# Convolution taps on TensorE, rotation tables from angles, and three projections as plain fp32 products

## The chip, the cores and the metric

The kernel runs on one core of one Trainium2 chip. Times are device microseconds (us) of that core, from the profiler or from timed runs; lower is better. The engines named here: PE is TensorE (matrix products; PEld is its weight loading, which overlaps), DVE is VectorE, ACT is ScalarE, POOL is GpSimd, and SP is SyncE, which issues nearly all transfers. TensorE runs at one of two clock levels, 1.2 and 2.4 GHz; the profile gives the granted clock of each stretch as a share of the higher one.

## The reference, cut to what matters

Two transformer blocks run one after the other on 256 tokens of 1024 features, in fp32.

```python
# block 1, first mixer
h = rmsnorm(x, norm_mix_g)
q, k, v, f, u_ssm, g_attn, g_ssm = split(h @ w_in)      # 512, 512, 512, 8, 512, 1024, 1024
q, k = rmsnorm(q per head), rmsnorm(k per head)
y_attn = forgetting_attention(q, k, v, f)                # 8 heads of 64
y_ssm  = s5(u_ssm, A, log_dt, B, C, D, w_glu)            # x_t = exp(A dt) x_{t-1} + Bbar u_t; y = Re(C x) + D u
x = x + (sigmoid(g_attn) * (y_attn @ w_proj_attn) + sigmoid(g_ssm) * (y_ssm @ w_proj_ssm)) @ w_out
x = x + moe(rmsnorm(x))                                  # 32 experts, top 2
# block 2, layer 0
u = x @ conv_w_in                                        # 768 values, 768 gates, 256 memory queries
h = a * sigmoid(gate)                                    # 768 channels
h = causal depthwise convolution of h, 31 taps per channel, + dw_b
y = concat(silu(layer_norm(h)), memory_attention(q_mem)) @ w_o[0]
x = layer_norm(alpha * x + y); x = layer_norm(alpha * x + moe(x))
# block 2, layer 1: the same with a blockwise causal attention in place of the convolution
```

## The kernel before, in words

The stages follow each other: first mixer (0 to about 265 us), experts of block 1, convolution layer (about 539 to 690 us), its experts, attention layer, its experts. A tile framework orders the instructions of each engine when the kernel is compiled: in program order where nothing waits, and otherwise by what its own cost model takes to be ready. `issue_after` adds an order that it has to keep.

**Weights.** All weights come as 1 MB slots of a ring, in the order of one plan, loaded by SP in order (`pump`, `take`, `done`): five slots while the first mixer's state space work is live, thirteen after it. A slot is loaded again when `done` has given it back. With `K.borrow = n` the next n slots given back are not loaded again but kept in `K.kept`.

**Split products.** The mixers' projections split each fp32 operand into a high and a low fp32r part and make three fp32r products of it (`mm3`, L165 to L167): high by high, high by low, low by high. `split_half` (L137 to L143) splits half a slot: ACT copies the high part, then DVE (L143) or, for the halves numbered in the set `POOL`, GpSimd (L141) subtracts. `dense(n)` announces 2n halves; three pairs of buffers hold the split halves.

**First mixer (`Mixer1.run`).** The transposed input times the norm gain gives `xg`, which is split into `L`. Then come the projections in the order u (state space input), q, k, v (`in_proj`, four halves each, 16 pairs of k tile and token tile, 48 products of 512 columns each), with the per-head norms of q and k on ACT and DVE and their transposes on PE (L1314). `s5_lanes` works out the powers of the state transition on DVE from dt and A, and is put behind the last split of the q projection. `s5_weights(hf)` (hf 0 or 1, half of the groups) builds the input and output matrices (DVE and POOL) and the table `tab` of cos and sin of n times an angle, n from 0 to 63: it starts from two columns and doubles five times, each time with two complex products on DVE (12 instructions, L991 to L996). Half 0's tables are built ahead of the loop, half 1's in it. The loop (about 94.5 to 212 us) takes steps of the gate projections (split products), of the state space scan and of the attention in the order of a fixed string (`M1_ORDER`). `split_rows` splits a block of gain rows on POOL (L1516 to L1522), ahead of the loop.

**Convolution layer (`conv`).** The projection goes in 14 halves (`col_proj`, L1707 to L1709, 24 products of 256 columns each): values and gates of channel tiles 0 and 1, of 2 and 3, then the memory queries, then tiles 4 and 5. Of the six tiles of 128 channels, `ASG = 'vgmmmv'` gives two to DVE (31 instructions of one tap each, L1803), one to POOL (L1814 to L1823), and three to PE: `stack` builds diagonal weight blocks from the taps, `shift` writes the tile to DRAM and reads it back four times, shifted by one token each, into a kept ring slot (L1840, L1843), and `taps_pe` makes 32 small products (L1850). A memory attention of four heads runs in the same stretch; `CONV_ORDER` fixes the order of steps. Then follow a layer norm over the channels and the output projection (`out_proj`, split products), where the low part of each finished tile is subtracted on POOL (L1966).

Of the kernel before, what the change touches and what calls it, by code (L numbers as in the profile page):

```python
# [21 lines left out]
class Core:  # L22
# [165 lines left out]

    def out_proj(self, L, order, outs):
# [90 lines left out]
POOL = {2, 4, 13, 17, 18, 23, 26, 27, 31, 32, 33, 38, 42, 44, 45, 50, 52, 53, 56, 64, 65, 68, 71, 72, 73, 74, 76, 79, 84, 86, 87, 90, 94, 95, 97, 98}  # L280
# [687 lines left out]
class Mixer1:  # L968
# [29 lines left out]
    def s5_lanes(self):  # L998
# [22 lines left out]
        v.scalar_tensor_tensor(an, n, -P2, an, op0=OP.mult, op1=OP.add)  # L1021
        v.tensor_scalar(an, an, 3.1415925, -3.1415925, op0=OP.min, op1=OP.max)
# [35 lines left out]
        self.bb, self.sn = bb, sn  # L1058
# [13 lines left out]
    def s5_weights(self, hf):  # L1072
# [32 lines left out]
        c, s = self.tab[:, 0], self.tab[:, 1]  # L1105
        v.memset(c[:, :, 0:1], 1.0)
        v.memset(s[:, :, 0:1], 0.0)
        v.tensor_copy(c[:, :, 1:2], self.sn[:, 3, ps, None])
        v.tensor_copy(s[:, :, 1:2], self.sn[:, 2, ps, None])
        n = 2  # L1110
        d1, d2 = t1.rearrange("p a b c -> p (a b c)"), t2.rearrange("p a b c -> p (a b c)")
        ph = sp.tile([128, 2, 8], FT, name="s_ph")
        while n < 64:

            p_ = [z[:, :, n - 1] for z in (c, s)]
            o_ = [z[:, :, 1] for z in (c, s)]
            self.cmul(v, ph[:, 0], ph[:, 1], p_[0], p_[1], o_[0], o_[1], d1[:, :8], d2[:, :8])
            f = [ph[:, i, :, None].to_broadcast([128, 8, n]) for i in range(2)]
            e = [z[:, :8 * n].rearrange("p (a b) -> p a b", a=8) for z in (d1, d2)]
            self.cmul(v, c[:, :, n:2 * n], s[:, :, n:2 * n], c[:, :, :n], s[:, :, :n], f[0], f[1], e[0], e[1])  # L1120
            n *= 2
# [125 lines left out]
    def run(self, close, spare):  # L1247
# [25 lines left out]
        K.dense(16)  # L1273
        o = K.bank2()
        run(K.in_proj(L, o))
# [11 lines left out]
        qn = T("qn", [128, 2, 512], tag="m_u")  # L1287
        hs, hr = T("hs", [128, 2, 8]), T("hr", [128, 2, 8])
# [194 lines left out]
class Block2:  # L1483
# [30 lines left out]
    def split_rows(self):  # L1514
        g, r = self.K.nc.gpsimd, self.rtmp
        g.tensor_copy(self.rows, r)  # L1516
        g.tensor_sub(r, r, self.rows)
        for i in range(1, 3):
            o = slice(32 * i, 32 * i + 32)
            g.tensor_copy(self.rows[o], r[o])  # L1520
        g.tensor_sub(r[o], r[o], self.rows[o])
        g.tensor_copy(self.rows[o], r[o])  # L1522
# [249 lines left out]
    def conv(self, L, mp):  # L1772
# [20 lines left out]
        def taps(c, lo=0, hi=31, o=None, first=True):  # L1793

            o = cT[c] if o is None else o
            for w in range(lo, hi):
                h = hT[:, c, w:w + 256]
                if w == 0:
                    v.tensor_scalar(o, h, dw(c, 0), col(c), op0=OP.mult, op1=OP.add)
                elif w == lo and first:  # L1800
                    v.tensor_scalar(o, h, dw(c, w), None, op0=OP.mult)
                else:
                    v.scalar_tensor_tensor(o, h, dw(c, w), o, op0=OP.mult, op1=OP.add)  # L1803
                if (w - lo) % 4 == 3:
                    yield

        def taps_pool(c, hi):

            o, u = cT[c], B[:, 1]
            for w in range(0, hi, 4):  # L1810
                n = min(4, hi - w)
                h = hT[:, c, w:w + 256]
                h = bass.AP(tensor=h.tensor, offset=h.offset, ap=[list(h.ap[0]), [1, n], [1, 256]])
                g.tensor_tensor(u[:, :n], h, self.dw[:, 31 * c + w:31 * c + w + n, None].to_broadcast([128, n, 256]), op=OP.mult)  # L1814
                if n == 4:
                    g.tensor_tensor(u[:, 0:2], u[:, 0:2], u[:, 2:4], op=OP.add)
                    n = 2
                for j in range(1, n):
                    g.tensor_tensor(u[:, 0], u[:, 0], u[:, j], op=OP.add)
                if w:  # L1820
                    g.tensor_tensor(o, o, u[:, 0], op=OP.add)
                else:
                    g.tensor_scalar(o, u[:, 0], col(c), None, op0=OP.add)  # L1823
                yield
# [37 lines left out]
        def project():  # L1862
            for i in range(4):
# [291 lines left out]
```

## Time and profile before

| what | us |
|---|---|
| median of 3 runs (1815.61 to 1818.11) | 1817.23 |
| the profiled execution, its own time | 1819.84 |
| its span, first to last instruction | 1818.0 |
| PE busy, share of the span | 1636.8 (90%) |
| DVE busy | 711.5 (39%) |
| ACT busy | 439.6 (24%) |
| POOL busy | 227.9 (13%) |
| weights read | 539.23 MB, 297 GB/s over the span |

The shares are averages over stages with different limits: in the expert stages PE is busy nearly throughout, while in the first mixer and in the convolution layer PE, DVE and POOL take turns in waiting for each other. Matmuls overlap in the array, so a busy PE is not a PE at its peak. In the views a releaser is the instruction whose end let a waiting one start.

### The profile page before, as it was taken

Reading aid. Unit: us, or ns where it says so; the run is one execution under the profiler, and the core shown is the slowest. Engines: PE = TensorE matmul, PEld = TensorE weight load, DVE = VectorE, ACT = ScalarE, POOL = GpSimd, SP = SyncE. Lnnn points to the kernel's source line nnn. Section 1 sums busy time; section 2 is a strip of 40 time slices with the busy share of each in tenths; the row PEclk is TensorE's granted clock in tenths of the full one; section 3 lists DMA queues with packets and bytes.
Section 4 is the critical chain, followed back from the end, with each engine's and each line's share of the span. In section 5 each row is a group of like instructions: output and inputs, shape, how many; then the busy total and the mean of one; then the engine's idle time right before and its main releaser. Section 6 shows DMA issues by size and latency. Waiting matters only on the chain. (4 is left out here: it accounts for less than half of the span.)

```text
span 1818.0 us, 28309 instructions
## 1 busy us (share of the span) xinstructions
PE 1636.8 (90%) x11151; PEld 986.3 (54%) x11153; DVE 711.5 (39%) x1688; ACT 439.6 (24%) x859; POOL 227.9 (13%) x151
## 2 busy tenths in 40 slices
PE   6689888999957778999999999699799999999995
PEld 5477667888847554444444443598444444444442
DVE  6988764233337973111111111554611111111113
ACT  4244342222223351111111111355211111111111
POOL 4525110000017420000000000322000000000000
PEclk9799899989979889999999999899899999999998
DMA  7222566989991536998899999734199999879970
GB/s 291 93 92 79 199 257 270 419 350 419 419 372 63 173 116 257 422 421 357 353 421 421 421 421 421 267 121 139 71 387 419 419 419 420 348 280 420 397 296 26
DMA packets 77565, 543.43 MB, mean 299 GB/s; under 512 B 8861, under 2 KB 11037, under 8 KB 12216
## 3 DMA queue, kind: packets, MB, share of 16 engines
q1 hardware_dynamic: 77224, 540.75, 74.3%
q8 instruction: 130, 2.13, 0.5%
q14 instruction: 67, 0.55, 0.1%
q10 hardware_dynamic: 144, 0.00, 0.0%
HBM read 539.23 MB, written 1.49 MB: 297 GB/s over the span
## 5 line engine op out<-in xcount | busy, mean ns | idle before, releaser
L564 PE MATMUL ps<-ring,bA 128*32 128x128 f32 (+1 forms) x3336 | 455.9, 440 | 4.5 <-DMA ring<-in_gu_dram 2.0
L564 PEld LDWEIGHTS ps<-ring,bA 128*32 128x32 f32 (+1 forms) x3336 | 162.0, 124 | 204.0 <-issue 176.3
L615 PE MATMUL ps<-ring,bF 128*64 128x512 f32 (+1 forms) x1248 | 217.1, 523 | 1.1 <-ACT bA L1556 0.6
L635 PE MATMUL d<-w,bB 128*128 128x256 f32 (+1 forms) x1016 | 206.8, 350 | 2.2 <-ACT w L625 2.2
L635 PEld LDWEIGHTS d<-w,bB 128*128 128x128 f32 x1016 | 154.6, 189 | 78.8 <-issue 49.7
L626 DVE SCALAR_TENSOR_TENSOR w<-ps,cs,w 128x512 fp32r<-128x512 f32 (+1 forms) x95 | 62.8, 661 | 286.0 <-ACT w L625 285.9
L615 PEld LDWEIGHTS ps<-ring,bF 128*64 128x64 f32 (+1 forms) x1248 | 74.7, 128 | 125.0 <-issue 108.9
L511 POOL CAST bD<-bC 128x1024 bf16<-128x1024 f32 (+1 forms) x17 | 20.2, 1191 | 931.6 <-PE ps L548 827.0
L599 DVE COPY bF<-ps 128x256 f32<-128x256 f32 x63 | 26.8, 425 | 276.5 <-PE ps L597 276.5
L625 ACT ACTIVATE w<-ps,cs 128x512 fp32r<-128x512 f32 (+1 forms) x95 | 58.4, 615 | 268.2 <-PE ps L615 268.2
L554 ACT ACTIVATE bB<-ps 32x256 fp32r<-32x256 bf16 (+1 forms) x127 | 47.6, 375 | 275.7 <-PE ps L548 260.7
L526 PE MATMUL ps<-bC,L 128*128 128x256 f32 x640 | 95.7, 297 | 11.9 <-PEq L655 7.6
L526 PEld LDWEIGHTS ps<-bC,L 128*128 128x128 f32 x640 | 88.1, 202 | 24.8 <-PEq L655 17.5
L528 ACT ACTIVATE bA<-ps 128x512 f32<-128x512 f32 x80 | 47.8, 597 | 200.5 <-PE ps L526 197.4
L137 ACT ACTIVATE W<-ring 128x1024 fp32r<-128x1024 f32 x66 | 69.4, 1056 | 110.1 <-PE d L167 39.4
L580 DVE SCALAR_TENSOR_TENSOR bE<-bE,ps 128x256 f32<-128x256 f32 (+1 forms) x95 | 33.6, 353 | 147.7 <-ACT bE L579 145.5
L166 PE MATMUL d<-W,L 128*128 128x512 f32 (+1 forms) x176 | 71.4, 406 | 21.7 <-DVE W L143 21.7
L141 POOL TENSOR_TENSOR W<-ring,W 128x1024 fp32r<-128x1024 f32 x27 | 65.9, 2445 | 148.8 <-ACT W L137 113.0
L165 PE MATMUL d<-W,L 128*128 128x512 f32 (+1 forms) x176 | 72.3, 415 | 11.8 <-ACT W L137 11.3
L579 ACT ACTIVATE bE<-ps 128x256 f32<-128x256 f32 (+1 forms) x95 | 31.3, 329 | 192.3 <-PE ps L564 192.3
L564 PE MATMUL ps<-W,bA 128*64 128x512 f32 (+1 forms) x472 | 70.4, 445 | 1.7 <-PEq L655 1.0
L167 PE MATMUL d<-W,L 128*128 128x512 f32 (+1 forms) x176 | 70.5, 402 | 0.0
(519 smaller groups left out, 2338.9 us busy)
## 6 DMA issues: line engine op xcount, KB each, us to landing
ring<-in_gu_dram SPq DMA_DIRECT2D x246, 1024.0 KB, 14.0
ring<-in_dn_dram SPq DMA_DIRECT2D x126, 1024.0 KB, 12.5
W<-in_gu_dram SPq DMA_DIRECT2D x38, 1024.0 KB, 13.7
x<-in_gu_dram SPq DMA_DIRECT2D x20, 1024.0 KB, 12.5
W<-in_dn_dram SPq DMA_DIRECT2D x17, 1024.0 KB, 13.0
ring<-in_w_in_dram SPq DMA_DIRECT2D x16, 1024.0 KB, 5.9
ring<-in_w_moba_dram SPq DMA_DIRECT2D x10, 1024.0 KB, 19.8
x<-in_dn_dram SPq DMA_DIRECT2D x9, 1024.0 KB, 17.0
```

Source lines behind the costliest of these rows:

```text
L137: copy = self.nc.scalar.activation(hi, s, AF.Copy)
L141: self.nc.gpsimd.tensor_sub(lo, s, hi)
L165: mm(out, lh, rh, start=start, stop=False, skip_group_check=True)
L166: mm(out, lh, rl, start=False, stop=False, skip_group_check=True)
L167: mm(out, ll, rh, start=False, stop=stop, skip_group_check=True)
L526: nc.tensor.matmul(p[:, i * n:i * n + n], x[:, t, k0 + i, :], g[t], start=s == 0, stop=s == 3)
L528: nc.scalar.activation(xg[:, k0:k0 + per, :], p[:, :per * n].rearrange("p (k c) -> p k c", k=per), AF.Copy)
L564: self.mm = nc.tensor.matmul(p[C * j:C * j + C, :2 * fw], xs(k), w[:, k % kk, :, fw * j:fw * j + fw], start=k == 0, stop=k == 7, skip_grou ...
L615: nc.tensor.matmul(p[C * j:C * j + C, :dw], hc[c], w[:, c % 2, dw * j:dw * j + dw], start=c == 0, stop=c == self.F // 128 - 1, skip_group_ ...
L625: nc.scalar.activation(hi, p[:, :dw], AF.Copy, scale=cs)
L626: nc.vector.scalar_tensor_tensor(lo, p[:, :dw], cs, hi, op0=OP.mult, op1=OP.subtract)
L635: nc.tensor.matmul(self.acc[t][dw * j // 512][:, dw * j % 512:dw * j % 512 + dw], S[:, j, 128 * t:128 * t + 128], y, start=False, stop=sto ...
```

## The change

Three projections of the first mixer (u, q, k) are made from unsplit operands: `in_plain` makes one plain fp32 product where `in_proj` made three fp32r products, straight from the ring slots. Their 12 halves are no longer split; `L` is filled later, for v and the gates. Half of the `xg` products move to ACT. `s5_lanes` is no longer put behind a split. The table of cos and sin is made from the angles: the angle is multiplied by n in two parts, reduced to one turn by seven or eight DVE instructions of 512 elements, and ACT takes the sine twice (once of a quarter turn less the absolute value). `split_rows` goes from POOL to ACT and DVE. In the convolution layer all six tiles go to PE, with six kept slots; the halves 50 to 68 that POOL split go to DVE, and so does the low part of the finished tiles (L1966), in two pieces.

```diff
+    def in_plain(self, L, outs):
+        for k in range(8):
+            if k % 4 == 0:
+                w = self.take()
+            c = 512 * (k % 4)
+            for t in range(2):
+                self.nc.tensor.matmul(outs[t], L[:, k, 128 * t:128 * t + 128], w[0][:, c:c + 512], start=k == 0,
+                                      stop=k == 7, skip_group_check=True)
+            if k % 4 == 3:
+                self.done(w)
...
-POOL = {2, 4, 13, 17, 18, 23, 26, 27, 31, 32, 33, 38, 42, 44, 45, 50, 52, 53, 56, 64, 65, 68, 71, 72, 73, 74, 76, 79, 84, 86, 87, 90, 94, 95, 97, 98}
+POOL = {2, 4, 13, 17, 18, 23, 26, 27, 31, 32, 33, 38, 42, 44, 45, 71, 72, 73, 74, 76, 79, 84, 86, 87, 90, 94, 95, 97, 98}
...
+        self.th = T("th", [128, 2, 16])
+        v.tensor_scalar(self.th[:, 0], an[:, 2], 6144.0, 6144.0, op0=OP.add, op1=OP.subtract)
+        v.tensor_sub(self.th[:, 1], an[:, 2], self.th[:, 0])
...
-        c, s = self.tab[:, 0], self.tab[:, 1]
...
-        while n < 64:
-            p_ = [z[:, :, n - 1] for z in (c, s)]
-            o_ = [z[:, :, 1] for z in (c, s)]
-            self.cmul(v, ph[:, 0], ph[:, 1], p_[0], p_[1], o_[0], o_[1], d1[:, :8], d2[:, :8])
...
-            self.cmul(v, c[:, :, n:2 * n], s[:, :, n:2 * n], c[:, :, :n], s[:, :, :n], f[0], f[1], e[0], e[1])
-            n *= 2
...
+        v.scalar_tensor_tensor(d1, it, -1.0, part(0), op0=OP.add, op1=OP.mult)
+        v.tensor_scalar(d2, d1, 1.0 / TWO_PI, 12582912.0, op0=OP.mult, op1=OP.add)
+        v.tensor_scalar(d2, d2, 12582912.0, None, op0=OP.subtract)
+        v.scalar_tensor_tensor(d1, d2, -P1, d1, op0=OP.mult, op1=OP.add)
+        v.scalar_tensor_tensor(d1, d2, -P2, d1, op0=OP.mult, op1=OP.add)
+        v.scalar_tensor_tensor(d2, it, -1.0, part(1), op0=OP.add, op1=OP.mult)
+        v.tensor_tensor(d1, d1, d2, op=OP.add)
+        v.tensor_scalar(d1, d1, 3.1415925, -3.1415925, op0=OP.min, op1=OP.max)
+        nc.scalar.activation(d2, d1, AF.Abs)
+        nc.scalar.activation(self.tab[:, 1], d1, AF.Sin)
+        nc.scalar.activation(self.tab[:, 0], d2, AF.Sin, scale=-1.0, bias=self.turn)
...
-            v.tensor_scalar(xg[:, k], self.xT[:, k], self.ng[:, k:k + 1], None, op0=OP.mult)
-            nc.scalar.activation(L[:, 0, k], xg[:, k], AF.Copy)
-            v.tensor_sub(L[:, 1, k], xg[:, k], L[:, 0, k])
+            if k % 2:
+                nc.scalar.activation(xg[:, k], self.xT[:, k], AF.Copy, scale=self.ng[:, k:k + 1])
+            else:
+                v.tensor_scalar(xg[:, k], self.xT[:, k], self.ng[:, k:k + 1], None, op0=OP.mult)
...
-        K.dense(16)
+        K.nsplit = 12
         o = K.bank2()
-        run(K.in_proj(L, o))
+        K.in_plain(xg, o)
...
+        for k in range(0, 8, 2):
+            nc.scalar.activation(L[:, 0, k:k + 2], xg[:, k:k + 2], AF.Copy)
+            v.tensor_sub(L[:, 1, k:k + 2], xg[:, k:k + 2], L[:, 0, k:k + 2])
...
-            run(K.in_proj(L, o))
+            K.in_plain(xg, o)
             if dst is qT:
-                with K.tc.issue_after(K.sub.ins):
-                    self.s5_lanes()
+                self.s5_lanes()
+            else:
+                K.dense(10)
...
-ASG = 'vgmmmv'
-POOL4 = 0
-STACK = 'vggvgv'
-CONV_ORDER = 'mpgppmpgmgvvgvvggppvpvpapvpvvapvavpvavpvmvapmvagpgagam'
+CONV_ORDER = 'kpkpkpkpkpppmmppkapapaapmapmaaaaamm'
...
-        g.tensor_copy(self.rows, r)
-        g.tensor_sub(r, r, self.rows)
+        nc.scalar.activation(self.rows, r, AF.Copy)
+        nc.vector.tensor_sub(r, r, self.rows)
...
+        K.borrow = 6 if l == 0 else 0
...
-        mt = [c for c in range(6) if ASG[c] == "m"]
-        K.borrow = len(mt)
         A = K.blk("A", [4, 8, 4, 32])
+        A = [A[:, i] for i in range(4)] + [B[:, 1].rearrange("p a (b c d) -> p (a b) c d", b=2, c=4), A[:, 0]]
...
-                    if ASG[2 * i + j] == "m":
-                        shift(2 * i + j)
+                    shift(2 * i + j)
...
-        proj, at, x, y, m = project(), attend(), on_vector(), on_pool(), on_tensor()
+        proj, at, st, m = project(), attend(), stacks(), taps()
         for i in CONV_ORDER:
-            next(dict(p=proj, a=at, v=x, g=y, m=m)[i], None)
+            next(dict(p=proj, a=at, k=st, m=m)[i], None)
...
-            g.tensor_tensor(tv(Y[:, 1, c]), nv(t), tv(Y[:, 0, c]), op=OP.subtract)
+            for h in range(2):
+                v.tensor_tensor(tv(Y[:, 1, c])[:, h], nv(t)[:, h], tv(Y[:, 0, c])[:, h], op=OP.subtract)
```

In the new order string k is a `stack`, p half of a channel projection, a a step of the memory attention and m the taps of one tile. The functions `taps` and `taps_pool` that made taps on DVE and POOL are gone.

## Rows read from the trace of the kernel before

**Rows 1.** Busy time by stretch, first mixer (us, busy and count by engine, clock, DMA)

```profile
10.10:24.70 14.60, 14.56 (x49) 11.05 (x49) 11.48 (x21) 8.96 (x19) 8.74 (x4) 1.00 1.02 397
24.70:43.60 18.90, 15.16 (x56) 12.35 (x57) 13.90 (x36) 7.15 (x10) 4.27 (x6) 0.82 0.67 248
43.60:73.70 30.10, 14.44 (x55) 10.33 (x54) 30.09 (x62) 7.71 (x11) 22.52 (x14) 0.66 0.15 48
73.70:94.50 20.80, 18.45 (x95) 14.44 (x95) 19.72 (x73) 7.96 (x12) 4.77 (x2) 0.92 0.50 182
94.50:212.00 117.50, 100.86 (x818) 81.43 (x817) 100.21 (x223) 46.55 (x83) 38.62 (x24) 0.94 0.24 82
```

**Rows 2.** PE's waits, 0 to 94.5 us (total, times, longest)

```profile
PE d L166 <- DVE W L143: 20.9, 3, 14.8
PE d L165 <- ACT W L137: 10.1, 1, 10.1
```

**Rows 3.** PE's waits, 94.5 to 212 us

```profile
PE ps L1204 <- DVE s_X L1187: 6.5, 1, 6.5
```

**Rows 4.** Timeline of PE, split products of the u projection (start, duration)

```profile
15.36 0.63 PE L167 MATMUL d<-W,L 128*128 128x512 f32 x1
...
22.27 0.39 PE L165 MATMUL d<-W,L 128*128 128x512 f32 x1
22.49 0.39 PE L166 MATMUL d<-W,L 128*128 128x512 f32 x1
```

**Rows 5.** Timeline of PE: 16 plain fp32 products of 256 columns, two records each

```profile
341.72 7.07 PE L1531 MATMUL ps<-ring 128*128 128x256 f32 x32
```

**Rows 6.** Timeline of ACT: the first two splits

```profile
9.01 1.99 ACT L137 ACTIVATE W<-ring 128x1024 fp32r<-128x1024 f32 x2
```

**Rows 7.** Timeline of DVE: first and last of the 60 table instructions of half 0

```profile
79.83 0.17 DVE L991 TENSOR_TENSOR s_u<-s_tab 128x8 f32<-128x8 f32 x1
...
99.54 0.42 DVE L996 TENSOR_TENSOR s_tab<-s_u,s_u 128x256 f32<-128x256 f32 x1
```

**Rows 8.** Groups of DVE instructions by shape, 70 to 80 us (busy, mean ns)

```profile
L1085 DVE TENSOR_TENSOR s_u<-s_bb,s_pw 128x512 f32<-128x512 f32 x2 | 1.4, 680 | 0.0
...
L143 DVE TENSOR_TENSOR W<-ring,W 128x1024 fp32r<-128x1024 f32 x1 | 1.2, 1219 | 0.0
```

**Rows 9.** Busy time by stretch, convolution layer, columns as in Rows 1

```profile
539.70:565.40 25.70, 25.70 (x193) 25.70 (x193) 12.74 (x12) 10.52 (x13) 13.31 (x8) 0.89 0.33 136
565.40:608.60 43.20, 27.73 (x161) 25.47 (x159) 42.70 (x36) 12.98 (x22) 40.42 (x30) 0.84 0.37 107
592.80:597.00 4.20, 1.75 (x14) 1.76 (x15) 4.17 (x4) 0.00 (x0) 3.96 (x4) 0.97 1.08 211
608.60:634.30 25.70, 20.62 (x237) 11.74 (x237) 22.46 (x45) 10.86 (x29) 3.56 (x2) 0.93 0.63 193
```

**Rows 10.** Timeline of PE: one projection half (24 products) apart, and taps of one tile

```profile
547.98 0.28 PE L1707 MATMUL d<-L,w 128*128 128x256 f32 x1
...
550.86 0.28 PE L1707 MATMUL d<-L,W 128*128 128x256 f32 x1
...
608.65 3.66 PE L1850 MATMUL ps<-ring,bA 128*32 128x256 f32 x64
```

**Rows 11.** Timeline of SP: tiles 2 and 3 to DRAM and back

```profile
584.43 0.81 SPq L1840 DMA_DIRECT2D h<-bD  x2
588.36 0.33 SPq L96 DMA_DIRECT2D ring<-in_dn_dram  x1
588.79 7.64 SPq L1843 DMA_DIRECT2D ring<-h  x8
```

**Rows 12.** Line 1843 (the reads back): time from issue to landing

```profile
DMA to landing us min/median/max: 6.4/7.2/8.5
```

**Rows 13.** ACT's waits, 655 to 665 us

```profile
ACT bC L1556 <- POOL L L1966: 2.0, 1, 2.0
```

**Rows 14.** PE's waits, 290 to 520 us, experts of block 1

```profile
PE ps L564 <- DMA ring<-in_gu_dram: 2.0, 2, 1.3
```

More of the change, by code (lines that the diff above doesn't have):

```diff
@@ L1057, in s5_lanes @@
         self.cmul(v, bb[:, 0], bb[:, 1], q("br"), q("bi"), c(f[:, 0]), c(f[:, 1]), w1, w2)
-        self.bb, self.sn = bb, sn
+        self.bb = bb
+        self.turn = T("turn", [128, 1])
+        v.memset(self.turn, TWO_PI / 4)
     def s5_alloc(self):
@@ L1103, in s5_weights @@
                         self.col("dd")[:, ps, None].to_broadcast([128, 8, 128]), op=OP.mult)
-        c, s = self.tab[:, 0], self.tab[:, 1]
[L1106 to L1112, printed above, removed]
-        while n < 64:
-            p_ = [z[:, :, n - 1] for z in (c, s)]
-            o_ = [z[:, :, 1] for z in (c, s)]
-            self.cmul(v, ph[:, 0], ph[:, 1], p_[0], p_[1], o_[0], o_[1], d1[:, :8], d2[:, :8])
-            f = [ph[:, i, :, None].to_broadcast([128, 8, n]) for i in range(2)]
-            e = [z[:, :8 * n].rearrange("p (a b) -> p a b", a=8) for z in (d1, d2)]
-            self.cmul(v, c[:, :, n:2 * n], s[:, :, n:2 * n], c[:, :, :n], s[:, :, :n], f[0], f[1], e[0], e[1])
-            n *= 2
+        d1, d2 = (z.rearrange("p a b c -> p (a b c)").rearrange("p (a n) -> p a n", a=8) for z in (t1, t2))
+        it = self.K.iota64[:, None, :].to_broadcast([128, 8, 64])
+        part = lambda i: self.th[:, i, ps, None].to_broadcast([128, 8, 64])
+        v.scalar_tensor_tensor(d1, it, -1.0, part(0), op0=OP.add, op1=OP.mult)
[9 more added lines that the diff above has]
+        nc.scalar.activation(self.tab[:, 0], d2, AF.Sin, scale=-1.0, bias=self.turn)
         g.tensor_copy(self.dec, self.mag4[:, ps, None].to_broadcast([128, 8, 64]))
@@ L1514, in split_rows @@
     def split_rows(self):
-        g, r = self.K.nc.gpsimd, self.rtmp
-        g.tensor_copy(self.rows, r)
-        g.tensor_sub(r, r, self.rows)
+        nc, r = self.K.nc, self.rtmp
+        nc.scalar.activation(self.rows, r, AF.Copy)
+        nc.vector.tensor_sub(r, r, self.rows)
         for i in range(1, 3):
             o = slice(32 * i, 32 * i + 32)
-            g.tensor_copy(self.rows[o], r[o])
-        g.tensor_sub(r[o], r[o], self.rows[o])
-        g.tensor_copy(self.rows[o], r[o])
+            nc.scalar.activation(self.rows[o], r[o], AF.Copy)
+        nc.vector.tensor_sub(r[o], r[o], self.rows[o])
+        nc.scalar.activation(self.rows[o], r[o], AF.Copy)
     def mem_kv(self):
@@ L1791, in need @@
                 next(proj)
[L1793 to L1824, printed above, removed]
-        mt = [c for c in range(6) if ASG[c] == "m"]
-        K.borrow = len(mt)
         A = K.blk("A", [4, 8, 4, 32])
+        A = [A[:, i] for i in range(4)] + [B[:, 1].rearrange("p a (b c d) -> p (a b) c d", b=2, c=4), A[:, 0]]
         dram = {}
         def stack(c):
-            (v if STACK[c] == "v" else g).tensor_tensor(
-                A[:, mt.index(c)], K.ident4[:, None, None, :].to_broadcast([128, 8, 4, 32]),
-                self.dx[:, c, :, :, None].to_broadcast([128, 8, 4, 32]), op=OP.mult)
+            v.tensor_tensor(A[c], K.ident4[:, None, None, :].to_broadcast([128, 8, 4, 32]),
+                            self.dx[:, c, :, :, None].to_broadcast([128, 8, 4, 32]), op=OP.mult)
         def shift(c):
@@ L1840, in shift @@
             nc.sync.dma_start(d, hT[:, c])
-            X = K.kept[mt.index(c)][0][:, :1136].rearrange("p (g t) -> p g t", g=4)
+            X = K.kept[c][0][:, :1136].rearrange("p (g t) -> p g t", g=4)
             for j in range(4):
@@ L1885, in attend, with stacks, taps @@
             yield from att.steps()
-        shared = ASG.rindex("v")
-        def on_pool():
+        def stacks():
             for c in range(6):
-                if ASG[c] == "g":
-                    need(c + 1)
-                    yield from taps_pool(c, 31)
-            if POOL4:
-                need(shared + 1)
-                yield from taps_pool(shared, POOL4)
-        def on_vector():
-            for c in range(6):
-                if ASG[c] == "v":
-                    need(c + 1)
-                    if c == shared and POOL4:
-                        yield from taps(c, POOL4, 31, z[:, 0])
-                        run(y)
-                        v.tensor_add(cT[c], cT[c], z[:, 0])
-                    else:
-                        yield from taps(c)
-        def on_tensor():
-            for c in mt:
                 stack(c)
                 yield
-            for c in mt:
+        def taps():
+            for c in range(6):
                 need(c + 1)
@@ L1920, in run @@
                 pass
-        proj, at, x, y, m = project(), attend(), on_vector(), on_pool(), on_tensor()
+        proj, at, st, m = project(), attend(), stacks(), taps()
         for i in CONV_ORDER:
-            next(dict(p=proj, a=at, v=x, g=y, m=m)[i], None)
-        for i in proj, at, x, y, m:
+            next(dict(p=proj, a=at, k=st, m=m)[i], None)
+        for i in proj, at, st, m:
             run(i)
```

6 lines of the change are left out of this document (2 added, 4 removed).

## The prediction, written before the run

> **What bounds the kernel now.** I read the page's busy shares first, then busy time by stretch, then PE's waits in the stretches where PE is not full, and last the timelines there. PE is busy 90% of the span, and in the expert stages it hardly waits: for all experts of block 1, transfers cost it 2.0 us [rows 14]. So what the change gives has to come out of the two stages that it touches, and a stage that ends earlier moves everything behind it by as much. In the first mixer the reader is to see PE at 14.44 of 30.10 us between 43.60 and 73.70, while DVE is full (30.09) and POOL works 22.52 [rows 1]. PE's waits say the same: 20.9 us for low parts from DVE (L143), one of them 14.8 long, and 10.1 us at the start for the first split [rows 2]. These splits were late because the state space work (`s5_lanes`) and the norms stand on the same engine. In the loop from 94.50 to 212.00 PE and DVE are about equally full, 100.86 and 100.21 of 117.50 [rows 1], and the longest wait is 6.5 us for the second scan on DVE [rows 3]. In the convolution layer PE is full until 565.40, then busy 27.73 of 43.20 us while DVE and POOL are full with taps (42.70 and 40.42), then 20.62 of 25.70 [rows 9].
>
> **The change part by part. First mixer, the three plain projections.** A split product of 512 columns starts every 0.227 us at the full clock (22.27, 22.49) [rows 4]; 48 of them make a projection, 10.9 us. The nearest row for a plain product of 512 columns is 16 plain ones of 256 columns in 7.07 us, 0.442 each [rows 5], so 0.884 for 512 (twice the columns; below 0.82 it would be fewer passes, which nothing shows). 16 of them are 14.1 us: PE pays 3.2 us more per projection, 9.7 in all. What goes is the wait. The first slot is in by 9.01, when ACT begins to split it [rows 6], so u can start at about 9.0 instead of 10.1. The first 5.7 us of the u projection ran at the 1.2 GHz level (products of 0.63 us, still at 15.36) [rows 4]; I let the new one start the same: 3.2 plain products there, 12.8 at the full clock, end at 26.0. q and k follow without a wait, since their slots come straight from the ring and the next stretch's transfers use only 0.67 and 0.15 of the queues' time [rows 1]: 32 x 0.884 = 28.3, end at 54.3. v is still split, 10.9 us, 65.2. What else PE does before 94.50 (transposes of q and k, forget gates) is at most the 14.44 + 18.45 us busy after 43.60 less two projections of 10.9, 11.1 us [rows 1]. So PE could be where it now is at 94.50 between 71 (half of that, the rest hidden in waits) and 76.3.
>
> DVE must keep up. It is busy 63.7 us from 24.70 to 94.50 [rows 1]. Off: eight low parts of q and k at 1.22 [rows 8], 9.8; the tables' 60 instructions between 79.83 and 99.54 [rows 7], of which I put 8 us before 94.50. On: eight table instructions of 512 elements, at 0.68 [rows 8] 5.4 (upper bound, those with one operand are shorter); four low parts of `L` of 512 elements, 2.7; two row subtractions of at most 1.22, 2.4. That is 56.4 us, from 24.70 to 81 if nothing else changes. But `s5_lanes`, no longer behind a split, can begin while DVE idles before 24.70 (11.48 of 14.60 busy), and POOL loses the row splitting, part of its 22.52 us, and with it some of the stretching of DVE's small instructions. I take 75.5 as the end of this part, halfway between PE's bound and DVE's: **19 us** gained; bounds 8 (DVE as stretched as now, 86) and 23.5 (PE alone).
>
> **The loop.** Half 1's doubling goes too: 60 instructions, half of them at 0.17 us and half growing to 0.42 [rows 7], so some 13 us of DVE, against 5.4. ACT takes three passes of 512 elements and reloads its functions at most twice more (sine and back). The 6.5 us wait for the scan should go [rows 3], the rest is PE's own work. I take **6 us**; bounds 0 (ACT's loads hit the softmax) and 14 (PE loses nearly all of its 16.6 idle us).
>
> **The convolution layer.** From 539.70 to 634.30 PE is busy 25.70 + 27.73 + 20.62 = 74.0 us [rows 9]. Three more tiles at 3.66 [rows 10] add 11.0, so 85.0; of it the part run at the lower clock goes if PE stays busy, at most 0.16 x 43.2 + 0.07 x 25.7 = 8.7 us (granted 0.84 and 0.93) [rows 9]. PE's floor is thus 76.3 to 85.0 of 94.6 us. The halves keep up: one every 2.88 us on PE [rows 10] against one DVE subtraction of 1.22 [rows 8] plus a stacking of as many elements; all taps of DVE and POOL go. The new wait is the trip through DRAM. For tiles 2 and 3 it ran from 584.43 to the last issue at 588.79 + 7.64 [rows 11] and 7.2 us more [rows 12], 19 us, with a 1 MB load issued ahead of the reads. Reading one tile four times is 0.58 MB, and the stretch with only such reads moved 211 GB/s [rows 9], so a pair of tiles is 5.5 us of transfer; with the write and the issues about 11 us where no load is ahead. Six slots are kept, so for the first pair none is. Cover for the first pair is three halves (8.6 us), for the last one tile of taps (3.66) and five attention steps. I put PE's idle time at 5 us in all, beside a floor of 79: 84, **10.5 us** gained; bounds 16 (floor and 2.6 us idle) and 0. Behind it, ACT waited 2.0 us for POOL's low part of the last tile [rows 13] with the output projection's last half queued behind on ACT; two DVE pieces take that wait away: **2 us**, bounds 0 and 2.
>
> A row about small transfers: the reads back have 1136 bytes per descriptor (284 values), and they moved 211 GB/s with the queues full (1.08) [rows 9]. The Trainium skill (DMA: Bandwidth & Descriptors, Specifications) says that transfers of at least 512 bytes reach line rate; the trace does not bear it out here. By that rule a pair would land some 2.6 us sooner, at the 397 GB/s that the first stretch moved [rows 1], and the sum would be up to 5 us better, two pairs having little cover; it goes by the row.
>
> Work on no path: the stacking (DVE has room, 12.74 of 25.70 busy [rows 9]), the copies of `split_rows` on ACT (7.71 of 30.10 busy [rows 1]), `xg` on ACT. Fewer slots are free for early loads in the convolution layer; three more slots are 7.9 us at those 397 GB/s and come back some 60 us before the experts start, so I cost them at nothing; if the ring were not full by then, it would cost those 7.9.
>
> **The sum.** 19 + 6 + 10.5 + 2 = 37.5. The profiled execution took 1819.84, 2.6 above the median of 1817.23; 1819.84 - 37.5 = 1782.3, in terms of the median 1780.
>
> **The rivals.** *More than forecast*: PE's floor is reached in both stages (23.5 + 12 + 15 + 2): 1765. For it: once splits are gone, DVE has few long runs ahead of PE. Against: both floors leave no idle time at all. *The DRAM trip is exposed*: taps wait for each pair as long as DVE's taps lasted; the convolution gives 0: 1790. For it: 19 us as seen [rows 11, 12]; against: no load stands ahead of the first pair. *DVE still paces the first mixer*, POOL's matrix work stretching `s5_lanes` as now: 8 + 3 there: 1794. *Slower*: PE's order, fixed at compile time, puts the taps of all three pairs ahead of projection halves that could run, and PE stands the whole trip each time, with loads ahead: 3 x 19 = 57 us on a floor of 79 is 136 instead of 94.6, 41 lost, against 27 won: about 1831. It decides from 14 us of standing per pair. Against it: PE ran three tiles' taps now with no wait put down to them. *The change gives nothing*: PE's 9.7 and 11.0 us more eat what the waits give back; it would need the waits of rows 2 to come back elsewhere: 1817.
>
> **How the numbers follow.** Forecast (1770 to 1790) 0.58; more 0.15; trip exposed 0.12; DVE paces 0.10; slower 0.03; nothing 0.02. The time is the forecast's, 1780. The range 1763 to 1800 takes in the first four but for their far ends (both of the smaller gains together would be 1804) and leaves out the rest, with the bounds' corners. About 0.2%, 3.6 us, is what a measurement of this kernel can tell from no change; faster by more 0.95, within 0.02, slower 0.03.
>
> **What would show it.** Right: in the profile after, plain products 0.44 us apart in two records each, k's end near 54, the loop starting near 75, no wait for L143 of over 3 us before it; sine loads on ACT in the loop and no wait for the second scan; POOL idle in the convolution layer, whose loop ends some 10 us sooner, with waits of PE on reads back of a few us; expert stages of the same length. Wrong: PE waiting for `L` or for norms after k; taps' PE waits of 10 us or more; an expert stage that begins with waits for weights; plain products much slower than 0.884 us, or at the lower clock for long.

## The result, and the profile after

The changed kernel takes 1796.91 us, the median of 4 runs (1795.08 to 1801.01), against 1817.67 for the kernel before beside it (1815.61 to 1821.64, 4 runs): a ratio of 0.9886, 95% interval 0.9869 to 0.9904. That is 20.8 us faster, where 37 was forecast. The profiled execution has a span of 1795.5 us, its own time is 1797.36.

Where the time came from is read from the start of the same instruction in the two timelines (one profile of each kernel):

| first start of | before | after | sooner by | by the forecast |
|---|---|---|---|---|
| the loop's work (transposes of the input matrices) | 94.7 | 82.7 | 12.0 | 19 |
| the gated unit behind the loop | 210.6 | 192.4 | 18.2 | 25 |
| the transposes ahead of the first mixer's last product | 233.6 | 218.1 | 15.5 | 25 |
| the convolution layer's transposes | 524.8 | 508.4 | 16.4 | 25 |
| its projection | 538.9 | 525.6 | 13.3 | 25 |
| its last sum over channels (last product) | 634.3 | 610.0 | 24.3 | 35.5 |
| the residual behind its output projection | 676.6 | 650.6 | 26.0 | 37.5 |
| the residual of the last experts | 1290.5 | 1263.1 | 27.4 | 37.5 |
| the end | 1818.0 | 1795.5 | 22.5 | 37.5 |

The convolution loop and its tail gave 24.3 - 13.3 + 1.7 = 12.7 us, the 12.5 that were forecast. The first mixer gave 15.5 of 25. Some 3 us went at the convolution layer's start, and 4.9 in the last expert stage.

Busy time by stretch, first mixer of the kernel after (columns as in [rows 1]):

```profile
8.40:42.80 34.40, 34.40 (x76) 14.99 (x76) 27.59 (x80) 10.77 (x24) 18.24 (x14) 1.00 0.85 326
42.80:55.50 12.70, 3.41 (x17) 2.87 (x17) 11.04 (x24) 7.18 (x10) 2.38 (x1) 0.61 0.07 15
64.50:82.70 18.20, 16.02 (x92) 12.87 (x91) 11.14 (x27) 9.31 (x14) 3.75 (x2) 1.00 0.32 117
82.70:192.40 109.70, 97.72 (x799) 79.57 (x797) 84.67 (x143) 48.06 (x85) 40.15 (x25) 0.94 0.25 87
```

PE is full to 42.80 and then stands for most of 12.7 us. Its timeline there:

```profile
8.39 34.42 PE L196 MATMUL d<-ring,bB 128*128 128x512 f32 x76 [8.39 <-DMA ring<-in_w_in_dram]
52.09 3.62 PE L1334 MATMUL ps<-cst,m_qn 128*64 128x128 f32 x16 [9.29 <-DVE m_qn L1328]
```

Each plain product leaves two records: the 76 are u, q and the first 6 products of k. Then PE waits 9.29 us for q's norm, because its order has q's 16 transposes in the middle of k. DVE and ACT in that time:

```profile
38.38 1.75 DVE L1007 TENSOR_TENSOR s_w<-m,s_f 128x256 f32<-128x256 f32 x1
40.51 1.22 DVE L1534 TENSOR_TENSOR bE<-bE,rows 128x1024 f32<-128x1024 f32 x1
43.92 1.22 DVE L1538 TENSOR_TENSOR bE<-bE,rows 32x1024 f32<-32x1024 f32 x1 [1.82 <-ACT rows L1537]
45.16 1.28 DVE L1323 TENSOR_REDUCE m_hs<-bF 128x8 f32<-128x512 f32 x2
47.59 2.20 DVE L288 SCALAR_TENSOR_TENSOR m_hrm<-m_hrq,m_hrm 128x16 f32<-128x16 f32 x1
51.35 1.28 DVE L1328 TENSOR_TENSOR m_qn<-d,m_hr 128x512 f32<-128x512 f32 x2
```

```profile
25.50 1.06 ACT L1533 ACTIVATE rows<-bE 128x1024 bf16<-128x1024 f32 x1 [0.85 <-DMA bE<-in_rows_dram]
41.77 2.12 ACT L1537 ACTIVATE rows<-bE 32x1024 bf16<-32x1024 f32 x2 [15.20 <-DVE bE L1534]
43.91 1.08 ACT L1322 ACTIVATE bF<-d 128x512 f32<-128x512 f32 x2
```

Read them together. q's products were done near 37.5 (64 of the 76 records). Its squares (L1322) are queued on ACT behind the copies of `split_rows` (L1537); these wait 15.20 us for a subtraction (L1534), which is queued on DVE behind `s5_lanes`. So the row block, moved off GpSimd, came between q's products and q's norm.

PE's waits in the convolution layer (columns: engine, tile, line and releaser; total, times, longest), and busy time in its last stretch:

```profile
PE d L1724 <- ACT L L228: 13.6, 1, 13.6
PE ps L874 <- ACT bC L864: 2.9, 1, 2.9
PE ps L1833 <- DMA ring<-h: 2.6, 1, 2.6
```
```profile
555.50:580.00 24.50, 24.50 (x297) 19.29 (x296) 8.98 (x14) 13.61 (x32) 0.00 (x0) 1.00 0.68 189
580.00:612.00 32.00, 25.82 (x276) 16.79 (x269) 5.08 (x11) 10.84 (x24) 0.00 (x0) 0.89 0.71 211
```

Against [rows 9], PE is full to 580, and only the last pair's trip through DRAM shows, as 2.6 us. The wait of 13.6 at the start was 10.5 before. SP's issues tell why; first the kernel after, then the one before:

```profile
495.52 7.84 SPq L96 DMA_DIRECT2D ring<-in_w_o_dram  x4
523.09 0.81 SPq L96 DMA_DIRECT2D ring<-in_gu_dram  x2
```
```profile
511.23 25.50 SPq L96 DMA_DIRECT2D ring<-in_w_o_dram  x4
```

Before, SP issued three of the four `w_o` loads, took a branch over the experts' spare code, and issued the fourth behind it (hence 25.50 us). Now all four stand ahead of the branch, some 2.5 us apart, and ACT, which waits for SP behind the branch, starts that much later. ACT's waits say so, again the kernel after and then the one before:

```profile
ACT W L137 <- SPq L700: 14.9, 1, 14.9
```
```profile
ACT W L137 <- SPq L688: 12.3, 1, 12.3
```

### The profile page after: what moved, and what is told of

It is laid out like the page before. It is cut to its first block, busy times and chain, and to the rows that moved or that the text cites. A ratio compares the mean times of both kernels' runs of the same rounds, so it can differ in the third digit from the quotient of the medians.

```text
span 1795.5 us, 28394 instructions
## 1 busy us (share of the span) xinstructions
PE 1640.6 (91%) x11295; PEld 975.4 (54%) x11297; DVE 631.5 (35%) x1525; ACT 441.2 (25%) x862; POOL 142.0 (8%) x96
## 5 line engine op out<-in xcount | busy, mean ns | idle before, releaser
L538 PE MATMUL ps<-bC,L 128*128 128x256 f32 x640 | 97.1, 300 | 14.6 <-PEq L667 10.7
L137 ACT ACTIVATE W<-ring 128x1024 fp32r<-128x1024 f32 x58 | 61.1, 1057 | 106.3 <-PE d L167 35.5
L143 DVE TENSOR_TENSOR W<-ring,W 128x1024 fp32r<-128x1024 f32 x40 | 50.2, 1260 | 52.6 <-ACT W L137 52.5
L564 DVE CAST bB<-ps 32x256 fp32r<-32x256 bf16 (+1 forms) x127 | 54.0, 426 | 25.9 <-ACT bB L566 19.1
L1724 PE MATMUL d<-L,W 128*128 128x256 f32 x160 | 47.4, 296 | 13.6 <-ACT L L228 13.6
L165 PE MATMUL d<-W,L 128*128 128x512 f32 (+1 forms) x144 | 58.0, 402 | 1.5 <-ACT L L1925 1.0
## 6 DMA issues: line engine op xcount, KB each, us to landing
W<-in_gu_dram SPq DMA_DIRECT2D x38, 1024.0 KB, 12.5
W<-in_dn_dram SPq DMA_DIRECT2D x17, 1024.0 KB, 12.2
```

Of the source, the lines that this page charges most:

```text
L137: copy = self.nc.scalar.activation(hi, s, AF.Copy)
L143: self.sub = self.nc.vector.tensor_sub(lo, s, hi)
L165: mm(out, lh, rh, start=start, stop=False, skip_group_check=True)
L538: nc.tensor.matmul(p[:, i * n:i * n + n], x[:, t, k0 + i, :], g[t], start=s == 0, stop=s == 3)
L564: nc.vector.tensor_copy(o, i)
```

## The experiments

All kernels were timed beside the kernel before on the same chip; ratios are to it. The runs fall into several groups, in which the kernel before had medians from 1817.67 to 1822.03, so kernels of different groups are compared by their ratios. The last three columns are read from each one's profile: start of the loop, start of the transposes ahead of the first mixer's last product, and the time from the convolution layer's first product to its last sum over channels.

| kernel | median us | ratio, 95% interval | loop | mixer | convolution |
|---|---|---|---|---|---|
| before | 1817.67 | | 94.7 | 233.6 | 95.4 |
| after | 1796.91 | 0.9886 (0.9869 to 0.9904) | 82.7 | 218.1 | 84.4 |
| after_again | 1800.43 | 0.9883 (0.9861 to 0.9906) | 83.2 | 218.6 | 84.1 |
| conv_only | 1812.18 | 0.996 (0.994 to 0.998) | 93.9 | 232.8 | 86.2 |
| mixer_only | 1804.05 | 0.991 (0.9889 to 0.9932) | 83.5 | 219.0 | 96.6 |
| split_uqk | 1799.42 | 0.9884 (0.9865 to 0.9904) | 92.6 | 223.8 | 84.4 |
| old_tables | 1803.16 | 0.9907 (0.9887 to 0.9927) | 83.1 | 228.0 | 86.3 |
| rows_pool | 1798.41 | 0.9879 (0.9857 to 0.99) | 84.6 | 219.8 | 84.1 |
| order | 1795.3 | 0.9855 (0.9828 to 0.9882) | 81.1 | 215.5 | 86.3 |
| rows_late_order | 1789.87 | 0.9832 (0.981 to 0.9854) | 77.3 | 209.0 | 86.3 |
| layout | 1793.07 | 0.9852 (0.983 to 0.9875) | 84.2 | 219.8 | 84.3 |
| conv_order | 1785.28 | 0.982 (0.9796 to 0.9844) | 76.5 | 208.2 | 83.3 |
| ca_late | 1783.92 | 0.9795 (0.9767 to 0.9824) | 76.4 | 208.2 | 83.3 |
| ca_held | 1786.83 | 0.9816 (0.979 to 0.9843) | 71.4 | 209.0 | 79.5 |

The theory: the first mixer's shortfall is DVE's queue, the rest is the start of the convolution layer and the last expert stage. The rival: the plain products or the transfers are to blame.

**The two halves of the change alone: conv_only and mixer_only.** The kernel before with the convolution's hunks, or with the first mixer's:

```diff
+POOL = {2, 4, 13, ..., 44, 45, 71, 72, ...}
+        K.borrow = 6 if l == 0 else 0
+CONV_ORDER = 'kpkpkpkpkpppmmppkapapaapmapmaaaaamm'
...
```
```diff
+        K.in_plain(xg, o)
+        nc.scalar.activation(self.tab[:, 1], d1, AF.Sin)
+        nc.scalar.activation(self.rows, r, AF.Copy)
...
```

> The kernel before with only the convolution layer's part of the change (all six tiles on TensorE, the halves and low parts on VectorE); the first mixer is left as it was. If the stages add up as the two traces read (convolution loop 10.9 us, its tail 1.7), about 1805 against 1817.7 before, with the experts behind it as long as before. If the some 5.6 us that the changed kernel loses in its last expert stage come from this part (six slots kept, other places in the ring), about 1810, and the last stage takes 527 instead of 521 us.

> The kernel before with only the first mixer's part of the change (plain u, q, k; tables from angles; rows split on ScalarE and VectorE). By the traces' marks 12.0 us ahead of the loop and 3.5 net through loop and output projection: about 1802. If a part of that is given back later because weights or branches do not keep up, 1805 to 1808. Rival: the gain is all the convolution's, 1812 or more.

They gave 7.0 and 15.1 us, 22.1 together where the whole change gives 20.8 and, run again, 19.2: within their intervals, some 4 us to either side, the halves add up. The mixer's half is as its marks said; the convolution's came short of its 12.6. Its stage took 86.2, its last expert stage 529.6 instead of 527.5, and its projection started 2.4 us later than before (541.3 against 538.9), with all four `w_o` loads ahead of SP's branch; mixer_only has the order of before there, and no loss. From the layer's transposes to its projection the twelve profiles with four loads ahead of the branch show 16.2 to 18.2 us, the kernel before 14.1 and mixer_only 13.6. PE's own branch at this place is no rival: it took 2.9 us in conv_only and 6.2 in mixer_only.

**Plain or split: split_uqk.**

```diff
-        K.in_plain(xg, o)
+        run(K.in_proj(L, o))
```

> The changed kernel with u, q and k as split products again (12 halves split, three products each), the rest of the change kept (tables from angles, rows off GpSimd, all of the convolution layer). Theory (the plain products give nearly all of the gain ahead of the loop): the loop starts at 92 to 95, total about 1808. Rival (the other parts of the change, VectorE's smaller load and s5_lanes, give it): the loop starts at 83 to 87, total 1797 to 1801.

The theory held for the loop's start, 9.9 us later, and the rival for the total: the time cannot be told from the changed kernel's. The loop lasts 105.6 instead of 109.7 (92.6 to 198.2). It has as many products (800 and 799 records), at a granted clock of 0.97 instead of 0.94: PE is busy 2.9 us less and idle 1.2 us less. At the mixer's end 5.7 us are left, at the start of the last experts 7.5, and the last expert stage, 529.1 us against 532.4 and 535.4 in the two profiles of the changed kernel, takes 3.3 to 6.3 us of that back. PE's waits show what replaces the norm:

```profile
PE d L166 <- DVE w L143: 7.0, 1, 7.0
PE ps L1329 <- DVE m_qn L1323: 6.7, 3, 3.4
PE d L166 <- DVE W L143: 5.5, 2, 4.5
```

**The tables: old_tables.**

```diff
-        v.scalar_tensor_tensor(d1, it, -1.0, part(0), op0=OP.add, op1=OP.mult)
...
+        while n < 64:
...
+            self.cmul(v, c[:, :, n:2 * n], s[:, :, n:2 * n], c[:, :, :n], s[:, :, :n], f[0], f[1], e[0], e[1])
```

> The changed kernel with the tables of cos and sin made by doubling again, as before. Theory by the forecast's terms (the tables' 60 small instructions cost VectorE some 2.6 us more ahead of the loop and 7.6 more in it, and TensorE waits for VectorE there): the loop is 4 to 8 us longer, total 1801 to 1805. Rival (VectorE has room for them, since it idles some 10 us between 55 and 83 and the loop is paced by TensorE): within 2 us of the changed kernel, 1797 to 1799.

The total is the theory's, the loop grew by more than its 4 to 8 us: it starts where it did, and takes 121.9 us instead of 109.7:

```profile
83.10:205.00 121.90, 101.29 (x811) 81.97 (x810) 95.69 (x200) 46.27 (x83) 40.75 (x25) 0.90 0.25 87
```

DVE does 11.0 us more there, and PE waits 6.4 us for the second scan again (2.3 in the changed kernel) and 5.6 for the forget gates (2.7). PE is idle 8.6 us longer, and busy 3.6 us longer, at a granted clock of 0.90 instead of 0.94. At the mixer's end the new tables are worth 9.9 us, more than the plain products.

**The row block: rows_pool.**

```diff
-        nc.scalar.activation(self.rows, r, AF.Copy)
-        nc.vector.tensor_sub(r, r, self.rows)
+        g.tensor_copy(self.rows, r)
+        g.tensor_sub(r, r, self.rows)
...
```

> The changed kernel with the splitting of the row block back on GpSimd. Theory (the row block's two subtractions and the copies queued ahead of q's norm made PE stand): q's norm comes 4.7 us sooner, PE's 9.3 us gap in k's products shrinks to some 4.6, the loop starts near 78 instead of 82.7, total 1792. Rival (VectorE is slowed by GpSimd, so more work on GpSimd costs what it frees): loop start within 1 us of 82.7, total 1796 to 1799.

The rival held. q's norm starts 2.9 us sooner, and then its instructions of 16 elements meet those of GpSimd:

```profile
46.75 1.97 DVE L285 TENSOR_TENSOR m_hrq<-m_hrm 128x16 f32<-128x16 f32 x1
50.11 2.20 DVE L286 SCALAR_TENSOR_TENSOR m_hrq<-m_hrq,m_hs 128x16 f32<-128x16 f32 x1
```
```profile
46.56 2.14 POOL L1538 TENSOR_TENSOR bE<-bE,rows 32x1024 f32<-32x1024 f32 x1
49.92 2.36 POOL L141 TENSOR_TENSOR W<-ring,W 128x1024 fp32r<-128x1024 f32 x1
```

They end where GpSimd's do, at 48.7 and 52.3, and take 0.17 elsewhere. So leaving the block on GpSimd would have gained nothing (the loop starts at 84.6 instead of 82.7 and 83.2, the totals cannot be told apart). Whether its place in the queues is the fault, the next two kernels show.

**The order alone, and with the row block behind k's norm: order and rows_late_order.**

```diff
-        for dst, gain in ((qT, gq), (kT, self.col("kg"))):
-            o = K.bank2()
-            K.in_plain(xg, o)
...
+        oq, ok = K.bank2(), K.bank2()
+        K.in_plain(xg, oq)
+        self.s5_lanes()
+        K.in_plain(xg, ok)
+        K.dense(10)
+        for dst, gain, o in ((qT, gq, oq), (kT, self.col("kg"), ok)):
...
+        with K.tc.issue_after(last.ins):
+            spare()
```

The last two lines, with `last` the product that ends k's norm, are only in the second kernel.

> The changed kernel with the order of issue changed alone: k's 16 products ahead of q's norm and transposes, so that TensorE's order no longer has q's transposes in the middle of k's products. Theory (the place of the transposes in the order fixed at compile time costs the gap): u, q and k run unbroken to about 52, v follows near 56, the loop starts near 75, total about 1789. Rival (VectorE paces the stretch whatever PE's order): the loop starts at 80 or later, total 1794 to 1797.

> The changed kernel with k's products ahead of q's norm and transposes (as in the run with the order changed alone), and with the splitting of the row block, still on ScalarE and VectorE, kept behind k's norm. Theory (VectorE's queue paces the stretch ahead of the loop: q's norm stood behind the row block and its 1.8 us wait for ScalarE, and is not stretched while GpSimd is idle): q's norm ends near 47 instead of 53, k's near 65 instead of 70.6, the loop starts near 76.5 instead of 81.1, total some 4 to 6 us below the changed kernel, about 1792. Rival (the row block only moves, its 4.7 us come back before the loop): loop start at 80 to 81, total as with the order alone, 1795.

With the order alone, the three projections run unbroken:

```profile
8.58 43.48 PE L196 MATMUL d<-ring,bB 128*128 128x512 f32 x96 [8.58 <-DMA ring<-in_w_in_dram]
70.20 3.59 PE L1333 MATMUL ps<-cst,m_qn 128*64 128x128 f32 x16 [8.54 <-DVE m_qn L1327]
```

But PE then stands 8.54 us for k's norm, and the loop starts at 81.1: the rival held, DVE is the pace. With the row block out of the way too, q's norm ended at 48.5, k's at 65.9, and the loop started at 77.3, near the 76.5 expected. The last steps of the two norms in that kernel:

```profile
47.18 1.28 DVE L1327 TENSOR_TENSOR m_qn<-d,m_hr 128x512 f32<-128x512 f32 x2
64.63 1.28 DVE L1327 TENSOR_TENSOR m_qn<-d,m_hr 128x512 f32<-128x512 f32 x2
```

The first mixer's end came 24.6 us sooner than before (209.0 against 233.6), nearly the 25 that the forecast had promised. Of the 9.1 us over the changed kernel, 5.4 come ahead of the loop, by the two orders, and 3.7 in it, where the granted clock was 0.97 instead of 0.94 and PE was busy 2.6 us less.

**The last expert stage: after_again and layout.** The first is the changed kernel unaltered. The second adds code that is never executed, so that later code of PE lies elsewhere:

```diff
         with tc.If(most > 0, label=f"rest{self.n}"):
...
+            if self.n == 0:
+                p = K.ps()
+                for _ in range(124):
+                    nc.tensor.matmul(p[:, 0:128], K.ident, K.ident, start=True, stop=True, skip_group_check=True)
```

> The changed kernel unaltered, once more, beside the two that follow. What belongs to the kernel should repeat: loop start near 82.7, convolution from its first product to the last sum over channels 84.4, the long branches of TensorE at the same places (5.1 at the convolution layer's start, 6.2, 2.7 and 2.1 in the last expert stage). What belongs to one execution should not: the time at the lower clock in the last expert stage (27.7 us of 453.5 in the first profile). Total 1796 to 1800.

> The changed kernel with 124 dummy products in a block of TensorE's code that is never executed (behind the experts of block 1), so that all later code of TensorE lies 247 instructions further on; no executed instruction differs. Theory (some branches over an expert's spare block are long because of where the code lies: 6.2, 2.7 and 2.1 us at the same three branches in three kernels with equal TensorE code length, and none of these in kernels of other lengths): these three branches go back to under 1 us, others may become long, the sum of TensorE's branches in the last expert stage changes by 3 us or more, and so does the time: 1791 to 1794 if none replaces them. Rival (the long branches come from the weights' traffic at that moment): the same branches stay long, total 1797.

The branches of PE over each expert's spare block in that stage (columns: shortest, median and longest in ns, first and last start), in the order before, after, after_again, layout:

```profile
L655 PEldq COMPARE_BRANCH  x33: 74/455/2486, 1315.6 to 1789.3; - x33
```
```profile
L667 PEldq COMPARE_BRANCH  x33: 74/451/6187, 1289.0 to 1766.6; - x33
```
```profile
L667 PEldq COMPARE_BRANCH  x33: 74/446/6187, 1289.6 to 1769.9; - x33
```
```profile
L667 PEldq COMPARE_BRANCH  x33: 74/436/2786, 1291.1 to 1769.3; - x33
```

In after_again the same branches are long as in the changed kernel's first profile (6.2, 3.0 and 1.8 us; 6.2, 2.7 and 2.1 there). In layout all three are short (0.4 to 0.5 us), another one takes 2.8, and PE's waits for branches from the stage's first gather to its last fall from 10.7 us to the 7.6 of the kernel before: 3.1 us that hang on where the code lies. Not all of it is a gain, for PE's idle time between these gathers is 20.4 and 21.4 us in the two profiles of the changed kernel, 18.8 in layout and 16.4 before. Nor is the code's place the whole cause: old_tables runs as many instructions on PE as the changed kernel, and there the longest of the three took 0.4 us. The ratio of 0.9852 fits, but its interval overlaps that of the changed kernel. The other part of the stage's loss is the clock. Between the same two gathers:

```profile
1302.40:1747.70 445.30, 428.89 (x2262) 194.97 (x2262) 83.69 (x201) 62.74 (x126) 7.29 (x7) 0.99 0.91 370
```
```profile
1275.00:1728.60 453.60, 433.18 (x2262) 197.50 (x2262) 83.86 (x201) 62.76 (x126) 7.29 (x7) 0.98 0.89 363
```

The first is the kernel before, the second the one after: 8.3 us longer, 4.3 of them busy and 4.0 idle. In the record of the granted clock 11.2 us of the first lie at 1.2 GHz, 20.0 of the second (not the 27.7 that the expectation of after_again names); in after_again 23.4 (456.3 us), in mixer_only 11.7 (445.9). Both profiles of the changed kernel lie high, but that is not shown to be its own: rows_pool (13.3) and order (23.4) differ from it in the first mixer alone and lie as far apart. Why the clock falls oftener in some executions was not settled. Behind the last gather the kernel after is 3.4 us shorter (66.9 against 70.3), which leaves 4.9 us lost in the stage.

**What is left: conv_order, ca_late, ca_held.** Each adds to the one before it, the first to rows_late_order:

```diff
-CONV_ORDER = 'kpkpkpkpkpppmmppkapapaapmapmaaaaamm'
+CONV_ORDER = 'kpkpkpkpkpppmmppkpppppaammaaaaaaamm'
```
```diff
-POOL = {2, 4, 13, 17, ...}
+POOL = {2, 4, 17, ...}
...
+        with self.K.tc.issue_after(behind) if behind else nullcontext():
+            self.s5_ca(ps)
```
```diff
-        with self.K.tc.issue_after(behind) if behind else nullcontext():
-            self.s5_ca(ps)
+        self.s5_ca(ps, behind)
...
+        if behind is not None:
+            g.tensor_copy(c1[:, 0, 0, 0:1], behind)
```

> The version with k's products first and the rows behind k's norm, and in the convolution layer all 14 halves of the projection ahead of the taps of channel tiles 2 and 3, so that tiles 4 and 5 start their trip through DRAM some 10 us earlier. Theory (what is left of TensorE's idle time in this stage is the last pair's trip and the attention's first softmax): the stage takes 80 to 81 instead of 84.4, no wait for the read back, total some 3 to 4 us below that version, 1786 to 1787. Rival (with the halves gone, the attention's waits for ScalarE have no cover): 84 or more, 1790 or more.

> The version before this one in the list, with GpSimd's 13 us of matrix work for the state space (seven instructions from 25.6 to 39.9) kept behind q's norm, and one half of v's weights split on VectorE in place of GpSimd. Theory A (whatever VectorE runs while GpSimd works is stretched): s5_lanes ends near 31.5 instead of 41.5 and q's norm near 45.5 instead of 48.4, but the stretch comes back on the instructions from 46 to 59, and the loop starts at 76 to 78 as without. Theory B (only short instructions suffer, the 512-element ones little): the loop starts near 74.5, total 2 to 3 us less.

> The version before, with GpSimd's matrix work really held: its first instruction now follows a one-column copy that reads q's normed values, so that the other six instructions and that one run behind q's norm (near 64 to 79 by the order on GpSimd). Theory (two-operand instructions of VectorE that meet a GpSimd instruction wait until it ends): the instructions of s5_lanes that took 1.2 to 1.8 us take 0.15 to 0.43, s5_lanes ends near 31.5 instead of 40.8; q's norm, now bounded by q's own products, comes 1 to 3 us sooner, the loop starts at 74 to 75.5, total 1 to 2 us less, unless the matrices come too late for their products near 82, which would cost some us. Rival (these instructions are long of themselves): durations and times as without.

conv_order: the wait for the read back, 3.4 us in rows_late_order, is gone. The stage takes 83.3 us instead of 86.3, between the theory's 80 to 81 and the rival's 84: PE is idle 3.7 us instead of 8.0, and busy 1.3 us longer. What is left is the clock: in ca_held, with the same code in this stage, PE is idle 3.8 us, the granted clock is 0.97 instead of 0.92, and the stage takes 79.5. The ratio cannot be told from that of rows_late_order. ca_late left its question open: `issue_after` orders the schedule, not another engine's run time, and GpSimd's matrix work stood at 25.9 to 40.1 as before; only one half went to VectorE, and the time did not change. In ca_held six of the seven instructions are really late (from 65.5 to 78.8). The same instruction of `s5_lanes`, first in ca_late, then in ca_held:

```profile
38.62 1.77 DVE L1007 TENSOR_TENSOR s_w<-m,s_f 128x256 f32<-128x256 f32 x1
```
```profile
31.50 0.42 DVE L1007 TENSOR_TENSOR s_w<-m,s_f 128x256 f32<-128x256 f32 x1
```

`s5_lanes` ends at 32.4 instead of 40.9, and the loop starts at 71.4. But the mixer's end did not move (209.0): the loop takes 111.9 us instead of 106.2. PE waits 3.6 us for ACT in its first steps, is idle 1.7 us longer in all, and busy 4.0 us longer at a granted clock of 0.92 instead of 0.97. Whether the loop's own chain or the clock is the limit there was not separated. The three versions cannot be told from each other; all beat both kernels, at 0.98 of the kernel before.

## Why the prediction was right in direction and too large

- **Convolution layer: right.** The stage was forecast at 84 us and took 84.4 and 84.1: PE busy 77.2 us where 79 were put down, and idle 7.2 where 5 were, so two small errors cancel, and that the number is so near is luck in part. The trip of the last pair, forecast at 11 us without a load ahead, took 12.4 to the first tap (586.71 to 599.07) with one ahead; the first pair's, at most 10.8 (544.72 to its first tap at 555.52), was hidden behind a full PE, as said. The tail gave 1.7 of 2. The Trainium skill's line rate from 512 bytes on (DMA: Bandwidth & Descriptors, Specifications) is again not borne out: from 549 to 553.5, with hardly anything but the first pair's reads back, the queues were busy 0.89 of the time at 192 GB/s.
- **Plain products: price right, worth wrong.** At the 2.4 GHz level the records start 0.429 us apart, 0.858 us a product (forecast 0.884); with the first ones, which ran at half that pace, the 38 took 0.906 each. But "q and k follow without a wait" failed: k ended at 64.5 instead of 54.3, since the order given to PE had q's transposes inside k (order shows 52.1 without them), and q's norm was late. By itself the exchange of split for plain is worth 5.7 us at the mixer's end, in one profile, and nothing that the total can tell.
- **The step that failed** is the end of the part ahead of the loop, "75.5, halfway between PE's bound and DVE's", with 19 us gained: 12.0 came. (Halfway between 71 and 81 would be 76, half a microsecond that changes nothing.) It was a sum of busy times on DVE; what counted was the place of q's and k's norms in its queue. The copies of `split_rows` were put down as work on no path; q's squares stood behind them on ACT. Both orders put right give 5.4 of the missing 7.0 us (rows_late_order, 77.3). The other mechanism there is that of the rival "DVE still paces the first mixer" (1794), nearest to the result: with GpSimd's matrix work out of the way of `s5_lanes` the loop starts another 5.0 us sooner (ca_held, 71.4 against 76.4 in ca_late), which the forecast had counted on only in part.
- **Loop: the size right (6.2 against 6), its make-up not.** The tables gave 12.2 us (old_tables), not the rest of a wait, and 2.3 us of the wait for the second scan are left; and 2.5 us were lost again behind the loop, where the output projection took 18.8 us from the gated unit's last product to the next transposes instead of 16.3, as PE now has fewer waits to fill with it: 14 of its 96 products stand ahead of the gated unit instead of 25.
- **Not in the sum:** 3.1 us at the convolution layer's start (one SP load issue ahead of a branch), and in the last expert stage 3.1 us of long branches and 4.3 us more of busy time with the clock lower. "Expert stages of the same length" failed in the last of the three.

So of the shortfall of 15 (37.5 against 22.5 between the profiles) 7.0 us lie ahead of the loop, 5.4 of them shown to be the place of q's and k's norms; 2.7 lie behind the loop, 3.1 at SP's branch, 4.9 in the last stage, and the stages between gained 2 to 3. The last stage's share differs between executions of one kernel (532.4 and 535.4 us).

## What to carry to other kernels

When splits or other long work are taken from an engine, ask what stands next in its queue, and walk the chain from each product to its consumer through every queue it passes: two short lists of rows, one for ACT and one for DVE, would have shown what q's norm stood behind. An instruction order fixed at compile time can put a late consumer in the middle of a run that is free to go; reorder first, then judge the arithmetic. A gain ahead of a loop is worth only what is left of it behind the loop: 9.9 us became 5.7 between split_uqk and the changed kernel, and 5.0 became nothing between ca_late and ca_held.

## What the hardware showed that was not expected

- DVE's instructions that read two tensors wait out a GpSimd instruction: 1.77 us for one of 256 elements that takes 0.42 alone, 2.20 for one of 16 elements that takes 0.17. The Trainium skill says so (SBUF — State Buffer, SBUF: two separate sides: the pair of ports that the two share is locked for the whole instruction); ca_held and rows_pool agree with it. The forecast had it as "stretching", priced only as a bound and in a rival.
- A branch of PE that jumps over a block of the last expert stage takes 0.45 us (median), and single ones 1.6 to 6.6. In the nine profiles of kernels that run as many PE instructions as the changed one, with no dead code ahead, two of them are the same ones every time, and the longest is the same one in eight, but 0.4 us in old_tables; dead code ahead moved all three away.
